# Four small moves in a hybrid transformer layer: mask order of attention's pv products, a weight split behind the input loop, two operand splits behind a unit's copies, and a last sum in halves

## The chip, the cores and the metric

The kernel runs on one core of a Trainium2 chip. A core has a matrix engine (TensorE, PE in the profile, with PEld for its weight loads), VectorE (DVE), ScalarE (ACT), GpSimd (POOL) and SyncE (SP), and 16 DMA engines. The metric is the device time of one execution in microseconds (us); less is better.

## The reference, cut to what matters

One layer over 1024 positions of width 1024, in float32: a normed input, one combined projection, two token mixers side by side, a gated merge, and a gated MLP with a convolution of width 3.

```python
h = rmsnorm(x, mix_norm[l])
q, k, v, su, sv, g_a, g_b = jnp.split(h @ w_in[l], splits, axis=-1)
y_att = sliding_window_attention(q, k, v, q_norm[l], k_norm[l], sinks[l])   # 8 q heads, 2 kv heads of 64, window 128
y_sgu = chunked_spatial_gating(su, sv, sgu_norm[l], w_s[l], b_s[l])         # u * (tril(W_s) @ rmsnorm(v) + b)
merged = (jax.nn.sigmoid(g_a) * (y_att @ w_oa[l]) + jax.nn.sigmoid(g_b) * (y_sgu @ w_ob[l]))
x = x + merged @ w_out[l]
x = x + conv_gated_mlp(rmsnorm(x, ffn_norm[l]), w_up[l], conv_w[l], conv_b[l], w_down[l])
```

In attention a block of 128 queries sees its own 128 keys and the 128 before, and inside these only keys at a distance of 0 to 127. The probabilities of the own block are therefore masked on one side of the diagonal, those of the block before on the other.

## The kernel before, in words

**Precision.** Every operand of a product is split in two fp32r tiles, a high part (`copy_hi`, an ACT copy, L89) and a low part (the operand less its high part, on DVE or POOL), and each product is three matmuls: high·high, high·low, low·high (`mm3`, L93 to L95, or `Blocks.prod`, L1061). `rsplit` (L193) is such a split of a raw weight tile, with the subtraction on POOL.

**Order.** PE's instructions stand in the order in which the code issues them. In the first stages the other engines are placed by a scheduler; in the branch products (`branch`) and from there on, every engine goes by the code's order. Each engine works its list off in order: an instruction that waits holds back those behind it.

**The input loop.** x comes in eight tiles. For each k, ACT and DVE split one tile of k and v weights (`wkv`, low part L230) and two halves of x (low part L234), PE adds the products to `pkv`, and `xsquare(k-1)` squares the tile before on ACT and adds the squares to `rstd_b` on DVE (L219). Behind the loop stand `xsquare(7)` and the split of the first u weights (`u0h` on ACT, `u0l` on DVE, L260). PE then sums the squares over partitions (`ssq`, L322), DVE copies them (L329), and the norms, and all later stages of attention, follow from that copy. The first q weights come in two tiles `rwq[0]` and `rwq[1]`, split at k = 5 and k = 6.

**Attention.** A unit is four of the query heads (a half) and one block b of 128 queries. `p_split` splits the transposed probabilities into `ch` (ACT) and `cl` (DVE, L497). POOL then makes four tiles, in this order: `eh` from `ch` (L504, the part that falls in the block of keys before), `ch` masked in place (L506), `el` from `cl` (L504), `cl` masked in place (L506). A unit with b = 0 has no block before it and no e tiles. `pv_mm` multiplies all of them with the values `vhl`: for each of two kv groups g, the products of ch, cl, eh, el are added in one half of a PSUM tile (L519).

**Branch products.** `branch(u, part)` makes unit u of `y_att @ w_oa` and `y_sgu @ w_ob` from seven block products of a 2×2 scheme. `first` computes A11·B11 (copied to `x1` by ACT, L1304), S3·T3 (copied to `x7`, L1306), A12·B21 and S1·T1, then DVE subtracts `x7` less `g1` (L622). `second` computes A22·T4, S2·T2, and S4·B22. The right-hand operands T1 to T4, B21, B22 are made by `y_split` (high part on ACT, low part on the engine given, L1232), in hooks between the units: `hooks[u, "x"]` runs behind the products of `first`, `hooks[u, 0]` behind the x7 subtraction, `hooks[u, 1]` at the end of `second`. The units' weights are split by ACT and POOL (`wjh`, `wjl`, L1290) one part ahead.

**The end.** The last of the MLP's down products, M3, is added to C12 by DVE, in four tiles d of 128×512 (`plus`, L1870), and each is stored by SP's queue (`put`, L1865).

Of the kernel before, what the change touches and what calls it, by code (L numbers as in the profile page):

```python
# [10 lines left out]
F = mybir.dt.float32  # L11
# [3 lines left out]
ALU = mybir.AluOpType  # L15
# [26 lines left out]
def body(ctx, tc, nc, a):  # L42
# [26 lines left out]
    def Z(s, dt, shape, off=16):  # L69

        return late_by(zr[0], "Z", s, dt, shape, off)
# [8 lines left out]
    def PH(s):  # L80
        if psum.get("H") is None:
            return PS(s)[:, 0:512]
        return psum["H"].tile([128, 512], F, tag="H", name=nm(s))
# [4 lines left out]
    def copy_hi(dst, src, scale=1.0):  # L88
        return nc.scalar.activation(dst, src, AF.Copy, scale=scale)  # L89

    def mm3(out, wh, wl, mh, ml, first, last, **kw):

        nc.tensor.matmul(out, wh, mh, start=first, stop=False, **kw)  # L93
        nc.tensor.matmul(out, wh, ml, start=False, stop=False, **kw)  # L94
        nc.tensor.matmul(out, wl, mh, start=False, stop=last, **kw)  # L95

    def wload(src, s, nk=8):
        r = raw(s)
        nc.sync.dma_start(r[:, :nk, :], src)
        return r  # L100
# [53 lines left out]
    vhl = at.tile([128, 8, 2, 128], R, name="vhl")  # L154
# [5 lines left out]
    wq = [Z("wq", R, (128, 2, 8, 256), 0)]  # L160
# [18 lines left out]
    def hx(j, k, c):  # L179

        h = c.start // 512
        return xq[k // 4][h][:, j, k % 4, c.start - 512 * h:c.stop - 512 * h]

    def rload(src, s):

        return [wload(src[:, c], s) for c in range(2)]

    def rsplit(w, r, c):

        rv = r.rearrange("p (k a) b -> p k (a b)", a=2)  # L190
        ks = slice(4 * c, 4 * c + 4)
        copy_hi(w[:, 0, ks, :], rv)
        nc.gpsimd.tensor_tensor(w[:, 1, ks, :], rv, w[:, 0, ks, :].bitcast(F), op=ALU.subtract)  # L193
# [9 lines left out]
    def xload(k):  # L203
        xr[k] = x_first[:, k, :] if k < 3 else pa.tile([128, 1281], F, tag="xr", name=nm("xr"), bufs=3)
        if k == 0:
            nc.sync.dma_start(xr[k][:, 0:513], a["xw"][k, :, 0:513])
            nc.sync.dma_start(xr[k][:, 513:1281], a["xw"][k, :, 513:1281])
        else:
            nc.sync.dma_start(xr[k], a["xw"][k])

    def xsquare(k):
        for c in (L, H):
            xs = xr[k][:, 257 + c.start:257 + c.stop]
            if k == 0:
                nc.scalar.activation(sqsum[:, c], xs, AF.Square)
                continue
            sq = PH("sq")
            nc.scalar.activation(sq, xs, AF.Square)
            nc.vector.tensor_tensor(sqsum[:, c], sqsum[:, c], sq, op=ALU.add)  # L219
# [7 lines left out]
    for k in range(8):  # L227
        x1 = xr[k]
        copy_hi(wkv[:, 0, k, :], x1[:, 1:257])
        nc.vector.tensor_tensor(wkv[:, 1, k, :], x1[:, 1:257], wkv[:, 0, k, :].bitcast(F), op=ALU.subtract)  # L230
        for c in xcuts[k] if k in xcuts else (slice(0, 512), slice(512, 1024)):
            xc = x1[:, 257 + c.start:257 + c.stop]
            copy_hi(hx(0, k, c), xc, scale=x1[:, 0:1])
            nc.vector.scalar_tensor_tensor(hx(1, k, c), xc, x1[:, 0:1], hx(0, k, c).bitcast(F),  # L234
                                           op0=ALU.mult, op1=ALU.subtract)
        for s in range(8):
            o = pkv[s // 4][:, (s % 4) * 256:(s % 4 + 1) * 256]
            c = slice(s * 128, (s + 1) * 128)
            mm3(o, hx(0, k, c), hx(1, k, c), wkv[:, 0, k, :], wkv[:, 1, k, :],
                k == 0 and s % 2 == 0, k == 7 and s % 2 == 1)  # L240
        if k > 0:
            xsquare(k - 1)
        if k + X_AHEAD < 8:
            xload(k + X_AHEAD)
        if k == 2:
            rwq = rload(a["wq"][0], "wq")
            nc.sync.dma_start(ident, a["ident"])
            nc.sync.dma_start(cp, a["cp"])
        if k == 4:
            u_raw = [wload(a["wu"][0], "wu")]  # L250
            nc.sync.dma_start(sink_b, a["sink"])
            nc.sync.dma_start(ali, a["ali"])
        if k == 5:
            rsplit(wq[0], rwq[0], 0)
        if k == 6:
            rsplit(wq[0], rwq[1], 1)
    xsquare(7)
    u_next = [wst.tile([128, 8, 128], R, tag="wh", name="u0h"), wst.tile([128, 8, 128], R, tag="wl", name="u0l")]
    copy_hi(u_next[0], u_raw[0])
    nc.vector.tensor_tensor(u_next[1], u_raw[0], u_next[0].bitcast(F), op=ALU.subtract)  # L260
# [60 lines left out]
    for s in range(8):  # L321
        nc.tensor.matmul(p_ssq[:, 2 * s:2 * s + 2], sqsum[:, s * 128:(s + 1) * 128], ones,  # L322
                         start=True, stop=True)
# [187 lines left out]
    def pv_mm(n):  # L511
        parts = st.pop(("p", n))
        p = PH("pv")
        for g in range(2):
            o = p[:, g * 256:(g + 1) * 256].rearrange("p (h q) -> p h q", q=128)
            gg = slice(2 * g, 2 * g + 2)
            ops = [(kb, w[:, gg, :]) for h_, l_, kb in parts for w in (h_, l_)]
            for i, (kb, w) in enumerate(ops):
                nc.tensor.matmul(o, vhl[:, kb, g, :], w, start=i == 0, stop=i == len(ops) - 1)  # L519
        st[("pv", n)] = p.rearrange("p (g h q) -> p g h q", g=2, q=128)  # L520

    def pv_out(n):
# [656 lines left out]
    yb = {"b": {}, "a": {}}  # L1179
# [5 lines left out]
    def y_src(br, n):  # L1185
        if (br, n) in y_raw:
            return y_raw[br, n]
        y = uT if br == "b" else yb["raw"]
        return y[:, 2 * (n[1] == "2"):2 * (n[1] == "2") + 2, L if n[2] == "1" else H]
# [32 lines left out]
            nc.sync.dma_start(t[:, i, :], d_ta[n])  # L1222
            y_raw["a", n] = t[:, i, :].rearrange("p (a b) -> p a b", a=2)

    def y_split(br, n, eng=nc.vector):
        i, j = Y_PLACE[br + n]
        if i not in y_slot:
            y_slot[i] = (U if i == 6 else Y)(f"y{i}", R, [128, 2, 4, 512])
        t = yb[br][n] = y_slot[i][:, j]
        src = y_src(br, n)  # L1230
        copy_hi(t[:, 0:2], src)
        eng.tensor_tensor(t[:, 2:4], src, t[:, 0:2].bitcast(F), op=ALU.subtract)  # L1232

    def ya_load():
        yb["raw"] = Y("ya", F)
# [3 lines left out]
    def gates():  # L1239
        q = v_end()  # L1240
        for c in range(1, 8):
            q = gate_pair(c, q)
        un["hooks"][0, "x"] = lambda: gates_end(q)
        un["hooks"][0, 0] = lambda: y_split("a", "B21", nc.gpsimd)
        un["hooks"][1, "x"] = lambda: y_split("a", "T3")
        un["hooks"][1, 0] = lambda: (y_split("a", "T4"), y_split("a", "T1", nc.gpsimd))
        un["hooks"][1, 1] = lambda: y_split("a", "T2", nc.gpsimd)
        un["hooks"][2, "x"] = lambda: y_split("a", "B22")

    def gates_end(q):  # L1250
        gates_close()
        th_load(0)
        gate_out(("a", 7), q.zv)
        q.last_sum()
        gate_out(("b", 7), q.zg)
# [37 lines left out]
    un = {"late": None, "hooks": {}}  # L1293
# [455 lines left out]
    def mlp():  # L1749
# [79 lines left out]
        X, Yb = [], []  # L1829
# [24 lines left out]
        rs = {}  # L1854
# [12 lines left out]
        def plus(n, d, p, last=False):  # L1867

            t = rs[n][:, d, :]
            nc.vector.scalar_tensor_tensor(t, p, 0.5, t, op0=ALU.mult, op1=ALU.add)  # L1870
            if last:
                put(n, d, t)

        def done(s):
            for d in range(4):
                if s == "M1":
                    nc.scalar.copy(Yb[d], X[d])
                if s == "M2":
                    plus("C11", d, Yb[d], True)
                if s == "M6":  # L1880
                    plus("C21", d, X[d])
                if s == "M7":
                    nc.scalar.activation(rs["x7"][:, d, :], Yb[d], AF.Copy, scale=0.5)
                if s == "M4":
                    plus("C21", d, Yb[d], True)
                if s == "M5":
                    plus("C22", d, X[d], True)
                if s == "M3":
                    plus("C12", d, X[d], True)
            if s == "M1":  # L1890
                y = U("res", F, [128, 2, 4, 512])
                res("C11", y[:, 0])
                res("C21", y[:, 1])
                rs["y"] = y
            if s == "M2":
                y = pools["yd"].tile([128, 2, 4, 512], F, name="res2")
                res("C22", y[:, 0])
                rs["x7"] = y[:, 1]
            if s == "M7":
                nc.vector.tensor_tensor(rs["C22"], rs["C22"], rs["x7"], op=ALU.add)  # L1900
            if s == "M4":
                res("C12", rs["y"][:, 0])
# [12 lines left out]
        prev, q, rms = first_pair()  # L1915
        for n in range(1, NPAIR):
            q = fast_pair(n, prev, q or Pair(n, lefts[n].w), (start0, start1, start), rms)
            prev, q, rms = q, None, None
        q = prev
        n_load = 4  # L1920
        for g in range(len(groups)):
            mms(g)
            s, k0, k1 = groups[g]
# [112 lines left out]
```

## Time and profile before

| | |
|---|---|
| time, median of 3 runs | 1186.83 us (1185.08, 1186.83, 1187.37) |
| the profiled execution's own time | 1185.6 us |
| its span in the profile | 1183.9 us |
| busy: PE, DVE, POOL, ACT | 1170.9, 874.8, 631.8, 566.3 us |
| granted TensorE clock | 1.00 |
| moved by DMA | 188.66 MB, mean 159 GB/s |

The profile is one execution, and its times are counted from the start of the span. A timeline row has start, duration, engine, line of the kernel, operation, output and inputs, and shape; a bracket behind it gives the idle time of that engine just before it, and what ended it. The durations of matmuls are modelled (they overlap): the distance from one start to the next tells how long one step takes.

### The profile page before, as it was taken

The page shows a single profiled execution, that of the slowest core. Times are in us where ns is not written, and L with a number is a line of the kernel's source. Part 1 is how long each engine was busy: PE and PEld are TensorE (multiplying, and loading weights), DVE is VectorE, ACT ScalarE, POOL GpSimd, SP SyncE. Part 2 cuts the span into 40 slices and gives each one's busy share as a digit, 9 for nine tenths or more (in the row PEclk, how much of TensorE's full clock was granted, in tenths as well). Part 3 has the DMA queues.
Part 4 walks back from the last instruction along what each step waited for, and adds up shares of the span by engine and source line. Part 5 has one row for each costly group of instructions (what it writes and reads, how often), then busy time and mean ns, then how long its engine had stood idle before and what let it go on. Part 6 is the DMA issues. An engine that isn't in the chain of part 4 may idle for free.

```text
span 1183.9 us, 15918 instructions
## 1 busy us (share of the span) xinstructions
PE 1170.9 (99%) x5842; PEld 991.5 (84%) x5842; DVE 874.8 (74%) x1036; ACT 566.3 (48%) x878; POOL 631.8 (53%) x435
## 2 busy tenths in 40 slices
PE   8999999999999999999999999999999999999998
PEld 8989989988888778888888888888888888888887
DVE  7798975743536877678788788877888797875674
ACT  8555667644346553335444444444344445425331
POOL 2367685488884764444867677776767540000000
PEclk9999999999999999999999999999999999999999
DMA  7010136257555654454555455454555268975471
GB/s 276 33 55 19 55 129 212 70 164 238 167 160 201 227 195 160 131 181 142 140 129 169 121 147 152 141 144 133 167 135 166 69 213 295 365 226 196 154 231 68
DMA packets 80798, 188.66 MB, mean 159 GB/s; under 512 B 9168, under 2 KB 16592, under 8 KB 80592
## 3 DMA queue, kind: packets, MB, share of 16 engines
q1 hardware_dynamic: 73008, 167.72, 41.4%
q0 software_dynamic: 7456, 15.73, 8.4%
q10 hardware_dynamic: 256, 4.19, 1.1%
q8 instruction: 46, 0.75, 0.3%
q14 instruction: 32, 0.26, 0.1%
HBM read 146.97 MB, written 49.02 MB: 166 GB/s over the span
## 4 chain that ended last, share of the span: by engine, by line
PE 83%; DVE 6%; issue 3%; DMA 2%; POOL 1%; ACT 1%; SPq 0%; DVEq 0%; POOLq 0%; ACTq 0%
PE pz L1061 50%; PE pdy L1850 8%; PE pd L1850 7%; PE px L95 2%; PE px L94 2%; PE px L93 2%; PE pvs L94 1%; PE pvs L93 1%; PE pvs L95 1%; DMA wj<-wb 1%; PE pq L93 1%; PE pq L95 1%; PE pq L94 1%; PE pv L519 1%; PE pu L95 1%
## 5 line engine op out<-in xcount | busy, mean ns | idle before, releaser
L1061 PE MATMUL pz<-T,qh 128*128 128x512 f32 x472 | 145.6, 390 | 0.0
L1061 PE MATMUL pz<-B,ph 128*128 128x512 f32 x352 | 109.5, 392 | 0.0
L1061 PEld LDWEIGHTS pz<-T,qh 128*128 128x128 f32 x472 | 88.4, 188 | 18.7 <-ACT u L886 0.3
L1020 POOL TENSOR_TENSOR pl<-lp,ph 128x1024 fp32r<-128x1024 f32 x30 | 73.1, 2437 | 53.0 <-ACT ph L89 53.0
L1061 PE MATMUL pz<-T,ql 128*128 128x512 f32 x236 | 91.8, 389 | 0.0
L1020 POOL TENSOR_TENSOR ql<-lq,qh 128x1024 fp32r<-128x1024 f32 x30 | 76.7, 2557 | 9.1 <-ACT qh L89 9.1
L1061 PEld LDWEIGHTS pz<-B,ph 128*128 128x128 f32 x352 | 65.2, 188 | 15.5 <-ACT x L1690 2.4
L1079 DVE TENSOR_TENSOR pz<-pz,rstd_b 128x1024 f32<-128x1024 f32 x60 | 73.9, 1232 | 4.6 <-ACT rstd_b L143 2.5
L1061 PE MATMUL pz<-T,s3h 128*128 128x512 f32 x232 | 71.4, 389 | 0.0
L1061 PE MATMUL pz<-y,wjh 128*128 128x512 f32 x224 | 69.4, 391 | 0.9 <-ACT x L1304 0.5
L1061 PE MATMUL pz<-B,pl 128*128 128x512 f32 x176 | 68.5, 389 | 0.0
L1850 PE MATMUL pd<-bh,ah 128*128 128x512 f32 x176 | 68.5, 389 | 0.0
L1850 PE MATMUL pd<-bl,ah 128*128 128x512 f32 x176 | 68.5, 389 | 0.0
L1850 PE MATMUL pd<-bh,al 128*128 128x512 f32 x176 | 68.5, 389 | 0.0
L1061 PE MATMUL pz<-T,AX 128*128 128x512 f32 x264 | 63.4, 389 | 0.0
L1061 PE MATMUL pz<-B,AX 128*128 128x512 f32 x264 | 63.4, 389 | 0.0
L1020 POOL TENSOR_TENSOR s3l<-lq,s3h 128x512 fp32r<-128x512 f32 x20 | 26.0, 1300 | 61.1 <-ACT s3h L89 61.1
L1061 PEld LDWEIGHTS pz<-T,AX 128*128 128x128 f32 x264 | 49.5, 188 | 10.3
L1061 PEld LDWEIGHTS pz<-B,AX 128*128 128x128 f32 x264 | 49.5, 188 | 10.3
L622 DVE TENSOR_TENSOR pz<-pz,u 128x512 f32<-128x512 f32 x37 | 25.9, 700 | 42.5 <-ACT u L1073 36.2
L89 ACT ACTIVATE ah<-ra 128x1024 fp32r<-128x1024 f32 (+1 forms) x24 | 23.7, 989 | 69.4 <-DMA ra<-wdown 22.1
L1545 DVE SCALAR_TENSOR_TENSOR tg<-pz,cp,tg 128x1023 f32<-128x1023 f32 (+1 forms) x44 | 56.2, 1278 | 0.8
(358 smaller groups left out, 3613.6 us busy)
## 6 DMA issues: line engine op xcount, KB each, us to landing
lp<-wup SPq DMA_DIRECT2D x22, 512.0 KB, 3.9
lq<-wup SPq DMA_DIRECT2D x22, 512.0 KB, 4.1
ra<-wdown SPq DMA_DIRECT2D x44, 256.0 KB, 4.7
b<-T SPq DMA_DIRECT2D x44, 256.0 KB, 3.5
lq<-wup POOLq DMA_DIRECT2D x42, 256.0 KB, 5.3
B<-tv SPq DMA_DIRECT2D x33, 256.0 KB, 2.0
T<-tt SPq DMA_DIRECT2D x33, 256.0 KB, 2.2
b<-B SPq DMA_DIRECT2D x33, 256.0 KB, 3.6
```

The costliest lines, as they stand in the source:

```text
L89: return nc.scalar.activation(dst, src, AF.Copy, scale=scale)
L93: nc.tensor.matmul(out, wh, mh, start=first, stop=False, **kw)
L94: nc.tensor.matmul(out, wh, ml, start=False, stop=False, **kw)
L95: nc.tensor.matmul(out, wl, mh, start=False, stop=last, **kw)
L519: nc.tensor.matmul(o, vhl[:, kb, g, :], w, start=i == 0, stop=i == len(ops) - 1)
L622: eng.tensor_tensor(out, x, y, op=op)
L1020: nc.gpsimd.tensor_tensor(l, r, h.bitcast(F), op=ALU.subtract)
L1061: nc.tensor.matmul(o, p[:, k, :], m, start=not more and k == 0 and j == 0, stop=k == nk - 1 and j == 2, skip_group_check=True)
L1079: nc.vector.tensor_tensor(z, z, rstd_b, op=ALU.mult)
L1545: nc.vector.scalar_tensor_tensor(t[:, j:], p[:, 0:1024 - j], cw[:, ci, 2 - j:3 - j], t[:, j:], op0=ALU.mult, op1=ALU.add)
L1850: nc.tensor.matmul(o[d], p[:, k - k0, m], q[:, k - k0, :], start=new and k == 0 and j == 0, stop=k == HK - 1 and j == 2, skip_group_check= ...
```

## The change

Four edits. No product and no mask is added or removed, and POOL's list of instructions stays in its order.

A. The split of `rwq[1]` stands behind `xsquare(7)` and no longer in the loop at k = 6. B. `pv_mm` runs over eh, ch, el, cl, each for both groups g, in place of ch, cl, eh, el for one group and then for the other. C. `y_split` is cut into `y_hi` and `y_lo`; T2's split and B22's high part go to `hooks[2, "x"]`, B22's low part to `hooks[2, 0]`. D. The last of the four C12 sums is made in two halves of 256 columns, the first stored by ACT's queue, the second by SP's.

```diff
         if k == 5:
             rsplit(wq[0], rwq[0], 0)
-        if k == 6:
-            rsplit(wq[0], rwq[1], 1)
     xsquare(7)
+    rsplit(wq[0], rwq[1], 1)
...
-        for g in range(2):
-            o = p[:, g * 256:(g + 1) * 256].rearrange("p (h q) -> p h q", q=128)
-            gg = slice(2 * g, 2 * g + 2)
-            ops = [(kb, w[:, gg, :]) for h_, l_, kb in parts for w in (h_, l_)]
-            for i, (kb, w) in enumerate(ops):
-                nc.tensor.matmul(o, vhl[:, kb, g, :], w, start=i == 0, stop=i == len(ops) - 1)
+        ops = [(part[2], part[j]) for j in (0, 1) for part in parts[::-1]]
+        for i, (kb, w) in enumerate(ops):
+            for g in range(2):
+                o = p[:, g * 256:(g + 1) * 256].rearrange("p (h q) -> p h q", q=128)
+                nc.tensor.matmul(o, vhl[:, kb, g, :], w[:, 2 * g:2 * g + 2, :], start=i == 0 and g == 0,
+                                 stop=i == len(ops) - 1, skip_group_check=True)
...
-        un["hooks"][1, 1] = lambda: y_split("a", "T2", nc.gpsimd)
-        un["hooks"][2, "x"] = lambda: y_split("a", "B22")
+        un["hooks"][2, "x"] = lambda: (y_split("a", "T2", nc.gpsimd), y_hi("a", "B22"))
+        un["hooks"][2, 0] = lambda: y_lo("a", "B22")
...
-                if s == "M3":
+                if s == "M3" and d < 3:
                     plus("C12", d, X[d], True)
+                if s == "M3" and d == 3:
+                    t = rs["C12"][:, d, :]
+                    for q, c in ((nc.scalar, slice(0, 256)), (nc.sync, slice(256, 512))):
+                        nc.vector.scalar_tensor_tensor(t[:, c], X[d][:, c], 0.5, t[:, c], op0=ALU.mult, op1=ALU.add)
+                        q.dma_start(a["out"][d, :, 512 + c.start:512 + c.stop], t[:, c])
```

On ACT, at the end of the input loop (`xr_209` and `xr_247` are x tiles 6 and 7, `wq_251` is `rwq[1]`; - is before, + is now):

```order
 L89 ACTIVATE x_6_119<-xr_209 128x512
-L89 ACTIVATE wq_102<-wq_251 128x1024
+L218 ACTIVATE sq_435<-xr_209 128x512
+L218 ACTIVATE sq_438<-xr_209 128x512
 L89 ACTIVATE wkv_120<-xr_247 128x256
 L89 ACTIVATE x_5_118<-xr_247 128x512
 L89 ACTIVATE x_6_119<-xr_247 128x512
-L218 ACTIVATE sq_437<-xr_209 128x512
-L218 ACTIVATE sq_440<-xr_209 128x512
-L218 ACTIVATE sq_443<-xr_247 128x512
-L218 ACTIVATE sq_446<-xr_247 128x512
+L218 ACTIVATE sq_441<-xr_247 128x512
+L218 ACTIVATE sq_444<-xr_247 128x512
+L89 ACTIVATE wq_102<-wq_251 128x1024
```

The q copy moved behind both of tile 7's squares, and tile 6's squares moved ahead of tile 7's splits.

On PE, one unit of pv, before:

```order
L519 MATMUL pv_2112<-ch_1994,vhl 128x256
L519 MATMUL pv_2112<-cl_1995,vhl 128x256
L519 MATMUL pv_2112<-eh_1998,vhl 128x256
L519 MATMUL pv_2112<-el_1999,vhl 128x256
L519 MATMUL pv_2112<-ch_1994,vhl 128x256
L519 MATMUL pv_2112<-cl_1995,vhl 128x256
L519 MATMUL pv_2112<-eh_1998,vhl 128x256
L519 MATMUL pv_2112<-el_1999,vhl 128x256
```

and now, where x2 stands for the two groups:

```order
L517 MATMUL pv_2112<-eh_1998,vhl 128x256 x2
L517 MATMUL pv_2112<-ch_1994,vhl 128x256 x2
L517 MATMUL pv_2112<-el_1999,vhl 128x256 x2
L517 MATMUL pv_2112<-cl_1995,vhl 128x256 x2
L93 MATMUL pu_2051<-x_3_116,wuh_1611 128x512
```

The first use of cl moved from the second product of the unit to the seventh of eight.

On ACT, around the third unit's first part (u_546 belongs to the second unit, x_561 and x_562 are the third unit's x1 and x7, `y<-ta` is T2, `y<-ya` is B22), before:

```order
L1325 COPY u_546_4221<-pz_4218 128x512
L89 ACTIVATE wjh_4298<-wj_4202 128x512
L89 ACTIVATE wjh_4298<-wj_4202 128x256
L89 ACTIVATE y_551_4263<-ta 128x1024
L1304 COPY x_561_4313<-pz_4311 128x512
L1306 COPY x_562_4314<-pz_4312 128x512
L89 ACTIVATE y_515_4063<-ya_3230 128x1024
```

and now:

```order
L1330 COPY u_546_4221<-pz_4218 128x512
L89 ACTIVATE wjh_4298<-wj_4202 128x512
L89 ACTIVATE wjh_4298<-wj_4202 128x256
L1309 COPY x_561_4311<-pz_4309 128x512
L1311 COPY x_562_4312<-pz_4310 128x512
L89 ACTIVATE y_551_4263<-ta 128x1024
L89 ACTIVATE y_515_4063<-ya_3230 128x1024
```

T2's high part moved behind both copies. On DVE at the same place, before:

```order
L1337 SCALAR_TENSOR_TENSOR m_4307<-th_4178,pz_4218 128x1024
L1232 TENSOR_TENSOR y_515_4063<-ya_3230,y_515_4063 128x1024
L622 TENSOR_TENSOR x_562_4314<-x_562_4314,pz_4311 128x512
L1324 TENSOR_TENSOR pz_4312<-x_561_4313,pz_4312 128x512
L622 TENSOR_TENSOR pz_4312<-pz_4312,u_563_4315 128x512
```

and now:

```order
L1342 SCALAR_TENSOR_TENSOR m_4307<-th_4178,pz_4218 128x1024
L621 TENSOR_TENSOR x_562_4312<-x_562_4312,pz_4309 128x512
L1233 TENSOR_TENSOR y_515_4063<-ya_3230,y_515_4063 128x1024
L1329 TENSOR_TENSOR pz_4310<-x_561_4311,pz_4310 128x512
L621 TENSOR_TENSOR pz_4310<-pz_4310,u_563_4313 128x512
```

B22's low part and the x7 subtraction have changed places.

More of the change, by code (lines that the diff above doesn't have):

```diff
@@ L1223, in ta_load, with y_hi @@
             y_raw["a", n] = t[:, i, :].rearrange("p (a b) -> p a b", a=2)
-    def y_split(br, n, eng=nc.vector):
+    def y_hi(br, n):
         i, j = Y_PLACE[br + n]
@@ L1229, in y_split, with y_lo @@
         t = yb[br][n] = y_slot[i][:, j]
-        src = y_src(br, n)
-        copy_hi(t[:, 0:2], src)
-        eng.tensor_tensor(t[:, 2:4], src, t[:, 0:2].bitcast(F), op=ALU.subtract)
+        copy_hi(t[:, 0:2], y_src(br, n))
+    def y_lo(br, n, eng=nc.vector):
+        t = yb[br][n]
+        eng.tensor_tensor(t[:, 2:4], y_src(br, n), t[:, 0:2].bitcast(F), op=ALU.subtract)
+    def y_split(br, n, eng=nc.vector):
+        y_hi(br, n)
+        y_lo(br, n, eng)
     def ya_load():
```

## Prediction

> **What bounds the kernel now.** The page comes first, then the list of what PE waited for, and then the timeline of each engine round those waits. In the page I look at how full PE is, in the list of waits at how much is left to win.
>
> ```profile
> span 1183.9 us, 15918 instructions
> PE 1170.9 (99%) x5842; PEld 991.5 (84%) x5842; DVE 874.8 (74%) x1036; ACT 566.3 (48%) x878; POOL 631.8 (53%) x435
> ...
> PE pv L519 <- POOL cl L506: 1.4, 3, 0.7
> ...
> PE pz L1061 <- ACT x L1304: 0.5, 2, 0.3
> PE pkv L95 <- DVE x L234: 0.5, 1, 0.5
> ...
> PE pz L1061 <- DVE x L622: 0.3, 1, 0.3
> ```
>
> The columns of a wait are total us, times, longest. TensorE is busy for 1170.9 of 1183.9 us, so all its idle time is 13.0 us, and the four rows that this change aims at hold 1.4 + 0.5 + 0.5 + 0.3 = 2.7 us of it. No matmul is added or removed: whatever the change wins is some of those waits, and a little behind the last matmul. The profiled execution took 1185.6 us, its span and 1.7 us around it; the median of the three runs, 1186.83, is 1.23 above that. I work in the time of the profile, and take the gain off the median at the end.
>
> **A: the second q split behind x.** The timelines of PE, POOL, DVE and ACT at the last input tile (start, duration, engine, line):
>
> ```profile
> 28.34 0.28 PE L94 MATMUL pkv<-wkv,x 128*128 128x256 f32 x1
> 29.09 0.38 PE L95 MATMUL pkv<-wkv,x 128*128 128x256 f32 x1 [0.47 <-DVE x L234]
> ...
> 25.07 2.83 POOL L193 TENSOR_TENSOR wq<-wq,wq 128x1024 fp32r<-128x1024 f32 x1 [1.08 <-ACT wq L89]
> ...
> 19.34 0.41 DVE L230 TENSOR_TENSOR wkv<-xr,wkv 128x256 fp32r<-128x256 f32 x1
> ...
> 25.52 0.67 DVE L219 TENSOR_TENSOR rstd_b<-rstd_b,sq 128x512 f32<-128x512 f32 x1
> 26.11 2.07 DVE L230 TENSOR_TENSOR wkv<-xr,wkv 128x256 fp32r<-128x256 f32 x1
> ...
> 28.30 1.40 DVE L234 SCALAR_TENSOR_TENSOR x<-xr,x 128x512 fp32r<-128x512 f32 x2
> 29.62 2.47 DVE L219 TENSOR_TENSOR rstd_b<-rstd_b,sq 128x512 f32<-128x512 f32 x4
> 32.02 1.21 DVE L260 TENSOR_TENSOR u0l<-wu,u0h 128x1024 fp32r<-128x1024 f32 x1
> ...
> 28.51 1.04 ACT L89 ACTIVATE u0h<-wu 128x1024 fp32r<-128x1024 f32 x1
> ...
> 31.72 1.84 PE L322 MATMUL ssq<-ones,rstd_b 128*128 128x2 f32 x16
> ...
> 33.60 0.17 DVE L329 COPY ss<-ssq 128x8 f32<-128x8 f32 x1 [0.37 <-PE ssq L322]
> ```
>
> Two such matmuls normally start 0.11 us apart; these start 0.75 apart, so 0.64 is lost, and a restarted first step costs another 0.11 (the next product stands 0.23 behind): 0.75 us. The cause is DVE's L230, which takes 2.07 here and 0.41 at 19.34, and which ends when POOL's split does (25.07 + 2.83 = 27.90). The split reads two tiles of SBUF, as L230 does; L219, at 25.52 under the same split, was not held (0.67). With the split moved away L230 ends near 26.5, and x(7)'s low half is there at about 27.2 to 27.8, before PE asks at 28.45. So the whole 0.75 goes.
>
> What is late next? ACT's work ahead of u0h is the same in sum, so u0h still starts at 28.51; the wq copy now stands right before it, and POOL's split runs from about 28.6 to 31.0. It is read from the fifth k of the q projection on, which begins at 33.4: not late. DVE's L219 sums, free of the split as at 25.52, finish near 30.2; u0l (two tiles of SBUF) waits until 31.0 and ends near 32.2, the two small constants behind it near 32.5. The copy of ssq is wanted at 33.60 − 0.75 = 32.85. That leaves 0.3 us, and everything behind hangs on this copy, so the gain is handed on. Were u0l held for a whole microsecond more, 0.7 of the 0.75 would be gone: the bounds of A are 0 and 0.75, and I take 0.75, since the only POOL work behind the split waits for this same chain.
>
> **B: the pv products in the order of the masks.** PE and POOL at the second and third of the three waits:
>
> ```profile
> 167.32 0.39 PE L519 MATMUL pv<-cl,vhl 128*128 128x256 f32 x1 [0.72 <-POOL cl L506]
> ...
> 168.25 0.28 PE L93 MATMUL pvs<-wv,x 128*128 128x256 f32 x1
> ...
> 178.59 0.39 PE L519 MATMUL pv<-cl,vhl 128*128 128x256 f32 x1 [0.39 <-POOL cl L506]
> ...
> 179.52 0.28 PE L93 MATMUL pvs<-wv,x 128*128 128x256 f32 x1
> ...
> 177.57 0.96 POOL L506 TENSOR_SCALAR_AFFINE_SELECT cl<-cl 128x512 fp32r<-128x512 f32 x1
> 178.51 2.86 POOL L193 TENSOR_TENSOR wvB<-z,wvB 128x1024 fp32r<-128x1024 f32 x1
> ```
>
> POOL makes eh, ch, el, cl. PE used cl as second of eight products, and then had six more to do; now cl is used by the last two. POOL's order is untouched, and it goes from one operation straight into the next here (windows below), so the mask comes when it came: 167.3 and 178.53. From the arrival of cl to the next matmul there were seven steps, 178.59 to 179.52, and there will be two: five steps of 0.115 = 0.57 us. The three waits do not add up, because what PE saves at one it waits for at the next: the gain left behind the third is 0.57.
>
> ```profile
> 158.00:182.00 24.00, 22.63 (x165) 20.77 (x164) 14.59 (x25) 14.93 (x29) 21.97 (x22) 1.00 0.46 165
> ```
>
> The columns are the window, its length, then PE, PEld, DVE, ACT and POOL busy, and the granted clock: POOL is busy for 21.97 of 24.00 us, more than any engine except PE. Below, B is bounded by 0 (masks that slip by 0.57 with a DVE operation that PE now releases sooner: the cl of 177.57 already took 0.96). Above, it is bounded by the 1.4 of the wait row and a restart each, 1.4 + 3 × 0.11 = 1.7, if the masks come sooner too. The POOL window is nearest to fixed masks: 0.57.
>
> **C: T2 and B22 behind the third unit's x7.** PE, ACT, DVE, POOL:
>
> ```profile
> 401.62 0.39 PE L1061 MATMUL pz<-y,wjl 128*128 128x512 f32 x1
> 402.32 0.72 PE L1061 MATMUL pz<-y,wjh 128*128 128x512 f32 x2 [0.31 <-ACT x L1304]
> ...
> 406.55 0.63 PE L1061 MATMUL pz<-y,wjh 128*128 128x512 f32 x2
> ...
> 407.70 0.39 PE L1061 MATMUL pz<-y,wjl 128*128 128x512 f32 x1
> 408.38 0.70 PE L1061 MATMUL pz<-y,wjh 128*128 128x512 f32 x2 [0.30 <-DVE x L622]
> ...
> 400.74 1.05 ACT L89 ACTIVATE y<-ta 128x1024 fp32r<-128x1024 f32 x1
> 401.69 0.57 ACT L1304 COPY x<-pz 128x512 f32<-128x512 f32 x1
> ...
> 404.37 3.26 DVE L1232 TENSOR_TENSOR y<-ya,y 128x1024 fp32r<-128x1024 f32 x1
> 407.56 0.68 DVE L622 TENSOR_TENSOR x<-x,pz 128x512 f32<-128x512 f32 x1
> ...
> 402.20 2.00 POOL L1290 TENSOR_TENSOR wjl<-wj,wjh 128x512 fp32r<-128x512 f32 x2
> 404.16 2.40 POOL L1232 TENSOR_TENSOR y<-ta,y 128x1024 fp32r<-128x1024 f32 x1
> ```
>
> At 402.32 PE waits for ACT's x1 copy, which stood behind T2's high half (400.74). Normal steps are 0.23, so 402.32 − 401.62 − 0.23 = 0.47 is lost, and 0.11 for the restart: 0.58. At 408.38 it waits for DVE's x7 − g1 (407.56), queued behind B22's low half, 3.26 us long because POOL splits T2 until 404.16 + 2.40 = 406.56: 408.38 − 407.70 − 0.23 = 0.45 lost, with the restart 0.5.
>
> Now x1 is copied from 400.74 to 401.3, and PE goes on at 401.85. x7 can be copied from 402.05, T2's high half follows until about 403.6: still ahead of POOL, which comes to T2 at 404.16, after its two splits, as before. So T2's low half comes at 406.56 as before, but PE, 0.58 earlier, wants it at 406.78 − 0.58 = 406.2. It waits 0.36, with notice and restart about 0.5: the first gain is nearly all given back there. DVE subtracts x7 − g1 at 404.4 to 405.1, far ahead of need, so the second stall of 0.5 is gone. B22's low half is queued at 405.1, held until 406.56 as before, and done near 407.65; PE wants it near 408.1. Net 0.58 − 0.5 + 0.5 = 0.6. Bounds: 0.35 (T2's notice dearer by half a step) and 1.1 (T2 not late).
>
> **D: the last sum in halves.** DVE's last sums and their stores, and rows of transfers (KB each, us to landing):
>
> ```profile
> 1177.88 2.73 DVE L1870 SCALAR_TENSOR_TENSOR res<-pd,res 128x512 f32<-128x512 f32 x4 [10.21 <-PE pd L1850]
> ...
> out<-res SPq DMA_DIRECT2D x16, 256.0 KB, 2.1
> ...
> taT<-yt SPq DMA_DIRECT2D x3, 512.0 KB, 2.9
> ...
> wb<-wb ACTq DMA_DIRECT2D x8, 512.0 KB, 3.9
> ...
> lq<-wup POOLq DMA_DIRECT2D x42, 256.0 KB, 5.3
> ```
>
> DVE ends at 1180.61, the store lands 2.1 later, and 1.2 us on the span ends. Two half sums should end about 0.08 later than one (one more start). A store of 512 KB took 2.9 for 2.1, so 256 KB more cost 0.8, and by that slope 128 KB less save 0.4; two halves at once take something from each other, so I estimate 0.3, net 0.2. Bounds −0.1 (a half lands no sooner, DVE's extra start stays) and +0.4. The Trainium skill, "DMA: Bandwidth & Descriptors", section "Issuing engines are not separate DMA queues", speaks against D: transfers begun by different engines run on the same 16 DMA engines and interleave. By it the two halves would land as one whole does, D would be about −0.1, and the time 0.3 above my forecast; no row here has two halves side by side.
>
> **The sum.** 0.75 + 0.57 + 0.6 + 0.2 = 2.1 us: profile 1185.6 to 1183.5, median 1186.83 to **1184.7**.
>
> **The rivals.** *The waits go without a successor.* T2 comes with PE or the masks do: A 0.75, B 1.7, C 1.1, D 0.2, together 3.7, so 1183.1. For it speaks that everything behind A starts 0.75 sooner, and masks and splits may hang on it. Against it: POOL is filled in the window at 158 to 182.
>
> *B22 loses its place.* DVE's B22 subtraction is held by T2 on POOL, and two wjl splits stand behind T2. Before, DVE got in at 406.56 (407.63 − 1.08). If instead both splits (2.00 us, as at 402.20) go first, it ends at 406.56 + 2.00 + 1.08 = 409.6, PE waits 1.5 and a restart: the gain is 2.1 − 1.6 = 0.5, 1186.3. Against it is the 404.37 row: it waited in the same way and came straight after T2. The Trainium skill, "SBUF — State Buffer", section "Who interferes with whom", says that the shared port pair is an exclusive lock, kept for the whole instruction by the one that starts first, and that a VectorE instruction with two SBUF inputs contends for it; the 2.07 and 3.26 rows agree, and by it DVE, waiting already, should go next.
>
> *Slower: the half on ACT's queue lands late.* The ACT queue has moved nothing near the end; its eight stores took 3.9, and a 256 KB load on POOL's queue 5.3. The first half is ready at about 1180.35; at 5.3 it lands at 1185.65 and not near 1182.5, so the end is 2.95 later than now: 0.75 + 0.57 + 0.6 − 2.95 = −1.0, 1187.9. It decides from 4.3 us to landing on. Against it: nothing else moves at the end, and the stores there take 2.1.
>
> That the order does not change as said is excluded by the program's own order.
>
> **How the numbers follow.** The forecast has 0.47, the waits that leave no successor 0.26, B22 0.16, the late half 0.11. A measurement of this kernel can tell about 0.2%, 2.4 us, from no change. My forecast lies just inside of that; with its bounds I put 0.22 of its 0.47 past it, so faster is 0.22 + 0.26 = 0.48, same 0.25 + 0.16 = 0.41, slower 0.11. The range goes from 1182.8 (3.7 and a little from D) to 1187.0 (the B22 case and the half microsecond by which a median of three lies off), and leaves out the late half and a few odd runs.
>
> **What would show it.** In the profile after: the L95 wait of pkv gone and L230 near 0.41 us; cl's waits only ahead of the seventh pv product, with two steps behind; no wait of pz for x L1304 or for DVE's x, and a new one of under half a microsecond for POOL's T2 near 405; the last landing under 2 us after DVE's end. It is wrong if the shift won at 29 is back by 40, if the masks move, if DVE's B22 subtraction ends past 408, or if ACT's store is the one that ends the span.

## The result

The changed kernel takes 1184.97 us (median of 19 runs, 1183.54 to 1186.36) against 1186.83 for the kernel before (19 runs, 1185.08 to 1187.70): a ratio of 0.9985, 95% interval 0.9978 to 0.9992, or 1.8 us less with 1.0 to 2.6 as bounds. The forecast was 1184.7, a gain of 2.1.

The two profiled executions differ by less: spans of 1183.5 and 1183.9. Single executions of one kernel scatter by 2 to 3 us, so the pair is compared place by place and not by its ends. The head of the page after the change:

```profile
span 1183.5 us, 15928 instructions
PE 1170.3 (99%) x5842; PEld 990.4 (84%) x5842; DVE 874.5 (74%) x1037; ACT 566.5 (48%) x878; POOL 631.8 (53%) x435
```

PE's list of waits after it (total us, times, longest):

```profile
PE pv L517 <- POOL cl L505: 1.0, 2, 0.5
PE pz L1060 <- ACT x L1695: 0.7, 1, 0.7
...
PE pm L93 <- ACT pm L926: 0.5, 1, 0.5
...
PE pz L1060 <- POOL y L1233: 0.3, 1, 0.3
```

pkv's wait for x and the two of the third unit (for x1 and for DVE's x) are gone. The one for T2's low half (POOL's y) is new and was forecast. The cl wait shrank from 1.4 to 1.0 us only. Two waits, at 218 (ACT's pm) and 592 (ACT's x), were not in the profile of before; both are taken up below (x there is a copy that the MLP's products wait for, pm a PSUM tile that ACT fills ahead of PE).

**A**, on DVE and POOL after:

```profile
26.32 0.41 DVE L230 TENSOR_TENSOR wkv<-xr,wkv 128x256 fp32r<-128x256 f32 x1
...
30.37 2.04 DVE L259 TENSOR_TENSOR u0l<-wu,u0h 128x1024 fp32r<-128x1024 f32 x1
...
33.28 0.17 DVE L328 COPY ss<-ssq 128x8 f32<-128x8 f32 x1 [0.68 <-PE ssq L321]
...
28.89 2.44 POOL L193 TENSOR_TENSOR wq<-wq,wq 128x1024 fp32r<-128x1024 f32 x1 [4.70 <-ACT wq L89]
```

L230 is back from 2.07 to 0.41 us. u0l now takes 2.04 us and not 1.21, and ends at 32.41, behind POOL's split (28.89 + 2.44 = 31.33); that u0l would wait for the split was forecast. DVE is still idle for 0.68 before the copy of ssq.

**B**, on POOL and DVE before:

```profile
176.87 0.64 POOL L504 TENSOR_SCALAR_AFFINE_SELECT el<-cl 128x512 fp32r<-128x512 f32 x1
...
177.10 1.97 DVE L622 TENSOR_TENSOR xa<-xa 128x512 f32<-128x512 f32 x2
```

and on PE, POOL and DVE after:

```profile
179.02 0.51 PE L517 MATMUL pv<-cl,vhl 128*128 128x256 f32 x2 [0.54 <-POOL cl L505]
...
176.84 1.09 POOL L503 TENSOR_SCALAR_AFFINE_SELECT el<-cl 128x512 fp32r<-128x512 f32 x1
178.00 0.97 POOL L505 TENSOR_SCALAR_AFFINE_SELECT cl<-cl 128x512 fp32r<-128x512 f32 x1
...
176.45 2.02 DVE L621 TENSOR_TENSOR xa<-xa 128x512 f32<-128x512 f32 x2
```

The cl mask ends at 178.97 and not at 178.53. DVE's two xa sums (differences of two halves of x for a later stage) started at 177.10 before, behind el's start, and only cl was slowed (0.96, in the prediction's rows); now they start at 176.45, ahead of el, and el takes 1.09 in place of 0.64 and cl 0.97.

**C**, on PE and DVE after:

```profile
405.97 0.50 PE L1060 MATMUL pz<-y,wjh 128*128 128x512 f32 x1 [0.26 <-POOL y L1233]
...
404.84 2.17 DVE L1233 TENSOR_TENSOR y<-ya,y 128x1024 fp32r<-128x1024 f32 x1
```

There is one stall in place of two. It costs 0.42 us: the step before it started at 405.32, and a normal step is 0.23. B22's low half ended at 407.01, straight after T2's, as before.

**D**, the last matmul before, then the last sums on DVE and the last matmul after:

```profile
1179.49 0.39 PE L1850 MATMUL pd<-bh,al 128*128 128x512 f32 x1
...
1179.52 0.76 DVE L1898 SCALAR_TENSOR_TENSOR res<-pd,res 128x256 f32<-128x256 f32 x2
...
1179.09 0.39 PE L1855 MATMUL pd<-bh,al 128*128 128x512 f32 x1
```

The transfers from 1179.9 on (KB, us to landing):

```profile
out<-res ACTq DMA_DIRECT2D x1, 128.0 KB, 2.1
out<-res SPq DMA_DIRECT2D x1, 128.0 KB, 2.1
```

A half lands in the 2.1 us that a whole tile took. From the start of the last matmul to the end of the span it was 1183.90 − 1179.49 = 4.41 us, and it is 1183.53 − 1179.09 = 4.44 now.

### The profile page after: what moved, and what is told of

The parts are those of the page before. It is cut to its first block, busy times and chain, and to the rows that moved or that the text cites. A ratio compares the mean times of both kernels' runs of the same rounds, so it can differ in the third digit from the quotient of the medians.

```text
span 1183.5 us, 15928 instructions
## 1 busy us (share of the span) xinstructions
PE 1170.3 (99%) x5842; PEld 990.4 (84%) x5842; DVE 874.5 (74%) x1037; ACT 566.5 (48%) x878; POOL 631.8 (53%) x435
## 4 chain that ended last, share of the span: by engine, by line
PE 82%; DVE 4%; POOL 3%; ACT 2%; issue 2%; DMA 1%; DVEq 0%; POOLq 0%; SPq 0%; ACTq 0%
PE pz L1060 50%; PE pd L1855 10%; PE pdy L1855 8%; PE px L95 2%; PE px L93 2%; PE px L94 2%; PE pu L95 1%; PE pu L93 1%; PE pu L94 1%; PE pv L517 1%; PE pq L93 1%; PE pq L95 1%; PE pq L94 1%; DVE xa L621 1%; DMA lq<-wup 0%
## 5 line engine op out<-in xcount | busy, mean ns | idle before, releaser
L89 ACT ACTIVATE AX<-lr 128x1024 fp32r<-128x1024 f32 x22 | 23.4, 1063 | 70.9 <-POOL lr L621 70.9
```

## The experiments

For each run I took PE's lead: the start of a matmul in the profile before, less that of the same matmul in the run. What counts is how the lead changes over a stretch, since a run's input loop alone may put it more than half a microsecond off. Each row is one execution, and the profile of before that all are compared with is one execution too.

| lead, us, at (time of before) | 28.3 | 31.0 | 142 | 160.5 | 181.9 | 212.7 | 219.1 | 395 | 412 | 492 | 580 | 600 | 612 | 1179 |
|---|---|---|---|---|---|---|---|---|---|---|---|---|---|---|
| the change | −0.36 | +0.33 | +0.11 | +0.64 | +0.23 | +1.39 | +0.64 | +0.60 | +1.24 | +1.22 | +1.21 | +0.23 | +0.05 | +0.40 |
| a_alone | −0.73 | −0.04 | −0.17 | −0.19 | −0.25 | −0.25 | −0.25 | −0.29 | −0.26 | −0.28 | −0.30 | −0.62 | −0.81 | −0.39 |
| b_alone | −0.38 | −0.48 | −0.53 | 0.00 | −0.44 | +0.72 | −0.02 | −0.06 | −0.04 | −0.07 | −0.10 | −0.10 | −0.15 | +0.27 |
| c_alone | −0.70 | −0.85 | −0.91 | −0.93 | −0.99 | −0.99 | −0.99 | −1.03 | −0.39 | −0.40 | −0.42 | −1.42 | −1.59 | −1.91 |
| d_alone | −0.68 | −0.78 | −0.94 | −0.97 | −0.93 | +0.23 | −0.51 | −0.55 | −0.53 | −0.53 | −0.56 | −0.97 | −1.15 | −0.73 |
| sums_alone | −0.48 | −0.44 | −0.50 | −0.49 | −0.10 | +1.07 | +0.32 | +0.29 | +0.34 | +0.32 | +0.32 | −0.79 | −0.97 | −0.60 |
| less_pe | −0.34 | −0.49 | −0.74 | −0.74 | −0.75 | −0.75 | −0.75 | −0.79 | −0.73 | +0.41 | +0.41 | −0.73 | −0.92 | −0.92 |
| abc_sums | −0.72 | −0.03 | −0.01 | +0.50 | +0.89 | +2.05 | +1.31 | +1.21 | +1.85 | +1.85 | +1.82 | +1.82 | +1.82 | +2.03 |
| after_again | +0.07 | +0.78 | +0.62 | +1.14 | +0.85 | +2.01 | +1.27 | +1.22 | +1.83 | +1.84 | +1.84 | +0.89 | +0.73 | +0.89 |
| abc_sums_again | −0.74 | +0.03 | −0.05 | +0.46 | +0.93 | +2.10 | +1.35 | +1.32 | +1.96 | +1.99 | +2.00 | +1.07 | +0.87 | +1.30 |

### Each part alone

The first four runs make one edit each and leave the other three as before; the diffs are the parts of the diff above.

a_alone:

```diff
-        if k == 6:
-            rsplit(wq[0], rwq[1], 1)
     xsquare(7)
+    rsplit(wq[0], rwq[1], 1)
```

> Only the second q split is moved. Both theories: the 0.75 us wait of pkv at 29 is gone and PE leads before by about 0.75 at once. 'Carried': the lead is still near 0.7 at 400 and at the end, time about 0.7 us below before. 'Reset': the lead is lost again, by 0.2 to 0.4 at the copy of ssq near 33, or wholly at the latest where the MLP waits for a chain that starts at a weight load (near 592), so the time is within 0.3 us of before.

Measured: 1185.71 against 1186.77, ratio 0.9995 (0.9986 to 1.0004). The lead grows by 0.69 between 28.3 and 31.0, where four of the five runs of the table with the old order lose another 0.10 to 0.15 (sums_alone gains 0.04). It still holds at 142 (−0.17 against −0.73) and at 580. So A is carried and worth 0.7 to 0.8; the time alone would not have shown it. The runs with the old order hold a surprise. Here is PE in c_alone:

```profile
29.04 0.38 PE L94 MATMUL pkv<-wkv,x 128*128 128x256 f32 x1 [0.36 <-DVE wkv L230]
29.89 0.38 PE L95 MATMUL pkv<-wkv,x 128*128 128x256 f32 x1 [0.47 <-DVE x L234]
```

There PE was early enough to wait for the held L230 itself, and lost 0.5 us more than the 0.75 (in d_alone 0.4). The table's column at 28.3 stands behind that wait and hides it. The same wait stands in less_pe and d_480, so in four of the seven profiles with the old order. In such executions A takes away about 1.2 us: less_pe and after_again enter the place within 0.1 us of each other (leads of 0.18 and 0.08 at 28.2), and at 31.0 they are 1.27 apart (−0.49 and +0.78).

b_alone:

```diff
-            ops = [(kb, w[:, gg, :]) for h_, l_, kb in parts for w in (h_, l_)]
+        ops = [(part[2], part[j]) for j in (0, 1) for part in parts[::-1]]
...
+            for g in range(2):
```

> Only the order of the pv products. 'Fixed masks' (the prediction): each cl mask ends when it did, and PE leads by 0.57 behind the third wait, near 179.5. 'Masks slip': DVE's xa sums (two SBUF operands), released by PE's earlier pv, start earlier and fall on el and cl of the third unit, which together take about 0.8 longer, so that cl ends near 178.9 and not at 178.5, and the lead behind the third wait is 0.1 to 0.2; the time is then that of before within 0.3 us.

Measured: 1186.55, ratio 0.9998 (0.9989 to 1.0006). The lead rises from −0.53 to 0.00 at the first of the three waits, and is −0.44 behind the third: 0.09 is won in all. POOL in b_alone:

```profile
177.50 1.09 POOL L504 TENSOR_SCALAR_AFFINE_SELECT el<-cl 128x512 fp32r<-128x512 f32 x1
178.66 0.97 POOL L506 TENSOR_SCALAR_AFFINE_SELECT cl<-cl 128x512 fp32r<-128x512 f32 x1
```

The masks slip, as the second theory said and by about its amount. These rows alone do not show that the sums are the cause; the runs without them, further down, do. The Trainium skill, "SBUF — State Buffer", section "Who interferes with whom", has a VectorE instruction with two SBUF inputs contend with a GpSimd instruction that reads SBUF; the sums read two such tiles, a mask reads one, and the masks' 0.64 became 1.09 and 0.97: the trace agrees.

c_alone:

```diff
-        un["hooks"][1, 1] = lambda: y_split("a", "T2", nc.gpsimd)
-        un["hooks"][2, "x"] = lambda: y_split("a", "B22")
+        un["hooks"][2, "x"] = lambda: (y_split("a", "T2", nc.gpsimd), y_hi("a", "B22"))
+        un["hooks"][2, 0] = lambda: y_lo("a", "B22")
```

> Only T2 and B22 behind the copies. Both theories: no wait for x1 at 402.3 nor for x7 - g1 at 408.4, a new one of about 0.4 us for T2's low half, PE leads by 0.56 at 410. 'Carried': 0.5 to 0.6 us below before at the end. 'Reset': the lead is gone behind 592 or 612, and the time is that of before within 0.3 us.

Measured: 1186.43, ratio 0.9994 (0.9985 to 1.0003). From 395 to 412 the lead grows by 0.64, in this run, in the change and in both runs of abc_sums (0.64); in after_again by 0.61. Behind 580 this run loses 1.0, which speaks for 'reset' at first sight; the section on the MLP below settles that.

d_alone:

```diff
-                if s == "M3":
+                if s == "M3" and d < 3:
...
+                    for q, c in ((nc.scalar, slice(0, 256)), (nc.sync, slice(256, 512))):
```

> Only the last sum in halves, behind everything. The prediction's sum: from the last matmul to the end of the span 4.2 us and not 4.41, time 0.2 us lower. Rival (transfers on the same 16 DMA engines): the second half lands as long after its issue as a whole tile did, 2.05 us, and DVE's extra start stays, 4.41 to 4.5 us, time the same within 0.1 us.

Measured: 1186.99, ratio 1.0004 (0.9995 to 1.0012). Its last matmul starts at 1180.21 and its span ends at 1184.67: 4.46 us against 4.41. The halves bring nothing.

### What a store's size costs

d_480 differs from d_alone in one line:

```diff
-                    for q, c in ((nc.scalar, slice(0, 256)), (nc.sync, slice(256, 512))):
+                    for q, c in ((nc.scalar, slice(0, 480)), (nc.sync, slice(480, 512))):
```

> The kernel before with the last sum cut into 480 and 32 columns: the last store holds 16 KB and not 256. If landing grows with the bytes (the prediction: 0.3 to 0.4 us for each 128 KB), it lands under 1.6 us after its issue, and from the last matmul to the end of the span passes about 4.0 us. If a store's landing is a fixed time at these sizes, it takes 2.0 to 2.1 again, and the end is 4.4 to 4.5 us behind the last matmul.

A single timing gave 1186.8 us, and the end lies 1185.10 − 1180.52 = 4.59 us behind the start of the last matmul: later than either side expected. The transfers at the end:

```profile
out<-res SPq DMA_DIRECT2D x1, 256.0 KB, 2.1
out<-res ACTq DMA_DIRECT2D x1, 240.0 KB, 2.1
out<-res SPq DMA_DIRECT2D x1, 16.0 KB, 2.2
```

The 16 KB land no sooner than the 256 KB, so at the end of this kernel a smaller last store wins nothing. That a store by itself takes a fixed time is not shown, because this one did not run alone. Between 1182.75 and 1183.5, packets of both queues moved side by side (packets, MB, share of 16 engines; q10 is ACT's queue with the 240 KB, q1 SP's with the 16 KB):

```profile
q10 hardware_dynamic: 107, 0.17, 62.5%
q1 hardware_dynamic: 144, 0.02, 16.1%
```

The Trainium skill, "DMA: Bandwidth & Descriptors", section "Anatomy of one DMA — SWDGE (gpsimd) path", has about 2.0 us fixed and a part that grows with the bytes, measured on GpSimd's path. The fixed part fits the 2.1 and 2.2 of these rows; the growing part, by an estimate with that formula 0.6 us for 256 KB, does not show in them, but here stores of neighbouring tiles overlap.

### Does the gain pass the MLP?

less_pe is the kernel before with a part of the computation left out, the low-high products of one branch unit:

```diff
+            q.terms = 2 if u == 5 else 3
...
-                for j, (p, q) in enumerate(((wh, 0), (wh, 1), (wl, 0))):
+                terms = ((wh, 0), (wh, 1), (wl, 0))[:self.terms]
+                for j, (p, q) in enumerate(terms):
```

> The kernel before, with the low-high term of one branch unit (the sixth) left out: 14 matmuls of 0.227, 3.2 us less PE work at about 460, ahead of the MLP. 'Carried': the whole lead of 3.2 passes 592 to 612 and the time is 2.9 to 3.4 us below before. 'Reset': the MLP's chain, which starts at weight loads, does not come sooner, PE waits near 592 for what it has won, and the time is at most 1 us below before.

Measured: 1185.31 against 1186.63, ratio 0.9989 (0.9980 to 0.9998): 1.3 us, which neither theory gave. PE in less_pe, at the next unit:

```profile
441.51 0.73 PE L1063 MATMUL pz<-y,wjh 128*128 128x512 f32 x2 [1.85 <-ACT x L1307]
```

Two of the 3.2 us are lost to a wait for the next unit's x1 copy on ACT, where the kernel before does not wait, and the lead grows by 1.14 from 412 to 492. The time is near that 1.14. At 592 this run loses another 1.0 at the step that waits; but c_alone loses 0.9 there with a lead of −0.42, and abc_sums, with +1.82, loses nothing while its repeat with +2.00 loses 0.8. That loss does not follow the lead, so it is not a place where gains are taken back. (The restart adds 0.1 to it in the table's column at 600.) It goes with one weight load. PE's row of the change, and the load on POOL's queue near 572 (KB, us to landing) in the kernel before, the change, abc_sums and abc_sums_again, in that order:

```profile
592.83 0.73 PE L1060 MATMUL pz<-B,ph 128*128 128x512 f32 x2 [0.68 <-ACT x L1695]
```
```profile
lq<-wup POOLq DMA_DIRECT2D x1, 256.0 KB, 4.7
```
```profile
lq<-wup POOLq DMA_DIRECT2D x1, 256.0 KB, 5.9
```
```profile
lq<-wup POOLq DMA_DIRECT2D x1, 256.0 KB, 4.7
```
```profile
lq<-wup POOLq DMA_DIRECT2D x1, 256.0 KB, 5.8
```

Over twelve profiles, that of d_480 among them, the load took 4.7 to 4.9 us where nothing was lost at 592 (three), 5.2 and 5.3 where 0.2 and 0.3 were (two), and 5.8 to 6.1 where 0.8 to 1.0 was lost (seven). The chain of work that ended last, in the change's profile, goes through this load, and on over ACT, POOL and DVE to the x copy that PE waits for:

```profile
571.64 5.90 DMA lq<-wup
577.62 0.64 ACT s3h L89
...
592.30 0.48 ACT x L1695
592.83 19.34 PE pz L1060 x84
```

It does so in c_alone and abc_sums_again too; before and in abc_sums PE runs on without a break there. The load itself starts with the lead: at 572.85 before, 1.21 us sooner in the change and 0.41 later in c_alone, whose leads at 580 are +1.21 and −0.42. So the chain comes sooner when PE does, against 'reset', and a slow load costs the same whatever the lead. What makes it slow in one execution is open. A smaller shift at 1000, −0.3 to +0.4 from run to run, does not follow the lead either.

### The sums out of the masks' way

sums_alone is the kernel before with this; abc_sums is parts A, B and C with this, and the last sum whole:

```diff
         if n == 18:
             x_gain(0, (2, 3))
-            x_sums((0, 1), True)
         if n == 19:
-            x_sums((2, 3), True)
+            x_sums((0, 1, 2, 3), True)
```

> The kernel before with only the first two xa sums moved one unit later. Third cl mask 0.64 and not 0.96 long, so the third wait of pv shrinks by 0.33 and PE leads by 0.3 between 142 and 182; if the sums are not what slows the masks, nothing changes.

> The change without its last part (the last sum whole again), and DVE's first two xa sums one unit later, so that they no longer stand beside the masks of the third waiting unit. 'Masks slip because of the sums': el and cl of that unit take 0.64 each, cl ends about 0.4 sooner than in the change alone, and PE's lead grows by 0.6 to 0.9 between 142 and 182 (0.1 in the change). With 0.7 of the q split and 0.64 of T2 and B22, about 2.2 us below before, 0.5 below the change. Rival: something else on POOL holds the masks (its wvB split), the lead there stays at 0.1 to 0.2 and the time is that of the change.

sums_alone took 1186.24 us in a single timing; its lead grows by 0.40 from 142 to 181.9, close to the 0.33 expected. abc_sums took 1184.33 against 1186.63, ratio 0.9980 (0.9971 to 0.9989). POOL and DVE there:

```profile
176.97 0.64 POOL L503 TENSOR_SCALAR_AFFINE_SELECT el<-cl 128x512 fp32r<-128x512 f32 x1
177.68 0.64 POOL L505 TENSOR_SCALAR_AFFINE_SELECT cl<-cl 128x512 fp32r<-128x512 f32 x1
...
180.62 2.50 DVE L621 TENSOR_TENSOR xa<-xa 128x512 f32<-128x512 f32 x4
```

Both masks take 0.64 again, and the lead grows by 0.90 from 142 to 181.9: 0.51 up to 160.5 and 0.39 behind it. sums_alone had 0.40 in all, so the order with undisturbed masks is worth 0.5, near the 0.57 that it was costed at, and the sums are what kept it from that. Then the change and this version again, side by side:

> The changed kernel once more, unaltered. If the wait of 0.84 us near 592 is a matter of the execution (a load that takes 4.7 or 5.9 us), another execution may well show it gone, and the lead behind 600 is then 1 to 1.3 us more than in the first profile; if it follows from the change, it is there again at 0.8 to 0.9. The waits at 29 (gone), 178 (el 1.09 and cl 0.97 long) and 405 (0.4) are the same in any case. Time again 1.2 to 2.2 us below before.

> The change without the halves and with the xa sums one unit later, beside the change itself on the same chip. By the leads so far (0.9 and not 0.1 for the pv part) it should be 0.6 to 0.8 us below the change, and 2.2 below before; el and cl of the third unit 0.64 each again. If the sums only move the cost elsewhere, it is within 0.3 us of the change.

The change took 1184.74 us, ratio 0.9987 (0.9978 to 0.9996). Its loss at 592 was there again (0.78; 0.84 in the first profile), so the first expectation's "may well show it gone" was a miss; that the loss belongs to the execution rests on the two runs of abc_sums. The pv part kept 0.23 us in it. abc_sums_again took 1183.99, ratio 0.9979 (0.9970 to 0.9988): 0.75 us below the change, as the leads of the pv part say (0.98 against 0.23), though the two intervals overlap. This version has the lowest times here.

## Why the prediction was right, and where it was not

- **A, 0.75: right**, with 0.7 to 0.8 in the traces. The row of L230 was read a little too simply: it ended at 26.11 + 2.07 = 28.18, 0.28 behind POOL's split and not with it. In executions where PE comes early A is worth 1.2, above the bound of 0.75: PE's own wait for L230 was no term of the sum. The bound at which u0l eats the gain was not reached.
- **B, 0.57: the step that failed** is "POOL's order is untouched ... so the mask comes when it came". The order was, the masks' length was not: PE's earlier pv released ya and with it the xa sums on DVE sooner, and these lie on el and cl. By the prediction's own sign ("it is wrong ... if the masks move") this part is wrong. The lower bound had the mechanism, with the cl of 177.57; it should have been the value taken, since the sums' start hangs on PE and the masks' does not. Worth 0.09 to 0.23 in the runs.
- **C, 0.6: right**, 0.61 to 0.64, with the new wait where it was forecast and a little shorter (0.42 in all, for about 0.5). The working charges the first wait 0.11 for the restart and the second almost none; with 0.11 for both it gives 0.64. The rival in which B22 loses its place did not come about in any of the five runs with C. The prediction's sentence on the Trainium skill ("SBUF — State Buffer", section "Who interferes with whom") takes from it that a lock is kept for the whole instruction; that section says so of VectorE's two-port modes, and for subtractions with two SBUF inputs what bears it out is that L230 and B22's low half (2.07 and 3.26 us) ended 0.28 and 1.07 us behind POOL's splits.
- **D, 0.2: wrong.** The slope came from a row of 512 KB stores; 128 KB landed no sooner than 256 KB. D measured −0.03 to −0.05, near the lower bound. The rule cited against it had the result right; whether sharing the engines is the reason no run shows. The last landing came 2.1 us behind DVE's end, where the prediction's sign was under 2. The half on ACT's queue was not late: 2.1 us. The eight transfers on that queue from which the rival took its 3.9 are no stores of a tile: `wb_copy` moves them from device memory to device memory.
- **The sum.** By the leads 0.7 + 0.1 + 0.64 − 0.03 = 1.4 us in the first profile, inside the measured 1.0 to 2.6. B and D were too high by 0.6 to 0.7 together, and what filled the gap to the measured 1.8, as far as it is more than scatter, was not forecast. A's worth in early executions may be part of it: 0.5 us in four of seven profiles would be 0.3 on average, an estimate from few executions. So may the pace of a stage described at the end, which gave this profile another 0.4. That the total came within 0.3 of the forecast is partly luck. No place in the MLP was found that takes a lead back as such.

## What to carry to other kernels

Where a product waits for a side engine's tile, ask not only whether that engine's order stays, but what else the earlier product will release, and whether that reads the same memory side by side with the tile's maker; here moving two sums that could wait by one unit was worth more than the reordering by itself (0.40 us against 0.09 to 0.23). A kernel that scatters by 2 us cannot be tuned by half microseconds with a dozen timings alone: the lead of each matmul over the same one of before shows them to about a tenth over a short stretch. Do not expect a cut store to land sooner, unless a row of that size says so.

## What the runs showed of the hardware that was not expected

Between 182 and 212 PE's step for 256 columns has one of two values, and each execution keeps to one of them there. Windows of before and after (PE busy with its count first; the clock, 1.00 in both, third from the end):

```profile
182.00:212.00 30.00, 30.00 (x257) 30.00 (x256) 17.93 (x27) 21.82 (x35) 13.64 (x12) 1.00 0.57 202
```
```profile
182.00:212.00 30.00, 30.00 (x267) 30.00 (x266) 18.49 (x27) 23.03 (x37) 13.19 (x12) 1.00 0.59 209
```

That is 257 matmuls against 267 in 30 us, 0.117 against 0.112 each, at the same granted clock and with PE never idle. It gives the change 1.2 us between 182 and 213; the wait for pm at 218 takes 0.75 of it back, so 0.4 stays. By the table of leads b_alone, d_alone, sums_alone, the repeat of the change and both runs of abc_sums gain the same 1.16 or 1.17 over this stretch (181.9 to 212.7), a_alone, c_alone and less_pe nothing. No edit has to do with the products of this stretch, and d_alone's comes only at the end of the kernel. But no kernel was seen at both paces: the two that were profiled twice ran at the faster one both times. So whether the pace belongs to the execution or to the program as built, and with that whether the 0.4 is part of what the change wins, these runs do not tell. What sets it is open.
